# One layer with routed experts on one core: expert work issued in source order, and GpSimd partition broadcasts replaced by TensorE products

## The chip, the core and the metric

One core of one Trainium2 chip runs the whole program. The metric is device time in microseconds of one execution; lower is better. TensorE multiplies (its weight loads are recorded apart), VectorE and ScalarE do elementwise work, GpSimd does some of it and issues the scatters, SyncE (SP) issues the loads.

## The reference, cut to what matters

All of it is float32. 512 latent tokens and 256 context tokens of width 1024 go through a modulated norm, an input projection, a recurrent half (RG-LRU) and an attention half, an output projection with a gated residual, and a second modulated norm. Then comes the part that reads nearly all of the bytes: each of 16 experts takes the 64 tokens that it likes best.

```python
aff = jax.nn.softmax((h @ w_router).astype(jnp.float32), axis=-1)
g, idx = lax.top_k(jnp.swapaxes(aff, 1, 2), cap)          # cap = 64 of 512, 16 experts
xe = jax.vmap(lambda hb, ib: hb[ib])(h, idx)
...
return (jax.nn.silu(xk @ wg) * (xk @ wu)) @ wd            # 1024 -> 2816 -> 1024
...
jnp.zeros((n, D), yb.dtype).at[ib.reshape(-1)].add(yb.reshape(-1, D))
```

Each expert has three matrices of 1024 x 2816 values, 34.6 MB together, which are read once.

## The kernel before, in words

**Who orders the work.** Up to the first expert, instructions are not issued as they are written: a class `Flow` records them, and `flush` (line 224) orders them by a list schedule with costs written in the code and issues them in that order on each engine. All of them carry line 254 in the profile. A partition broadcast is costed there by its length alone (line 219). There are three flushes: norm 1 and the first chunk (line 574); projections, LRU, attention and the early half of the output projection (line 1007); the rest of the output projection, the second norm and the router (line 1098). A fourth (line 1241) takes the expert choice and the first expert's gathering, gate, up and gate-value products. The later experts are not recorded: they are issued as they are written, and the tile framework's own scheduler orders them, by line numbers 1152 to 1234.

**Broadcasts.** `gp.partition_broadcast` copies a row to all partitions on GpSimd at five places: `nlam` (line 633, the attention's lambda), the residual's gate row for the early token tiles (`residual_gate`, line 954, called at 1003 into a tile `qT` of the attention) and again for the late ones (line 1022, `m2row`), the router's bias `brt` (line 1034) and the row by which the experts' outputs are scaled (lines 1149 and 1150, into `brow`). GpSimd also makes `rs`, the reciprocal root of a token tile's mean square (`rstd`), for each of the four tiles, from a sum `s`: a scaling and a power. The router's logits `lg` of a tile need `rs`, `brt` and the router product `pl`; softmax, a transpose `pT` and the search for the 64 largest (`largest`, line 1069, rounds of 8 on VectorE, results `tops`, `last`, `least`) follow. Token tiles 0 and 1 are projected early, beside the attention; tiles 2 and 3 late (`late_proj`, line 1036), in two PSUM banks `po`.

**Loads.** The experts' weights go through a ring of 14 slots (line 351) of 128 x 3072 values. A slot holds 128 rows of gate or of up (`load_ex`, line 368), or three blocks of 128 rows of down (`load_dn`, line 1155); an expert takes 16 and 8 slots. SP issues them in order and waits at each for its slot. Two slots (`ring`) come free early, four (`r`) with the end of the attention, four (`ring`) with the output projection, two more after it, and the last two, for the seventh pair of gate and up rows, with `least`, the end of routing. From then on a slot comes free when TensorE has multiplied what is in it.

**An expert.** `gather` (line 1166) makes one-hot columns for the tokens of two experts and multiplies them with the tokens `X1` (TensorE, four products for each of eight blocks of 128 channels, alternating between two PSUM banks `y` and `tr`; ScalarE writes the block to `xe`). `up_part` (line 1202) multiplies, for each block k of 128 channels, the 64 token columns with 128 rows of gate and of up, in six chunks of up to 512 columns; gate goes to partitions 0 to 63 of a bank and up to 64 to 127. A float32 product is recorded as two TensorE records. In the recorded first expert, a bias in the code puts block k of gathering just ahead of block k of gate and up. `gates` (line 1184) gathers the gate values. `down_part` (line 1214) takes SiLU and product by chunk, four transposes each into `hT`, and then all 44 down products (two halves of the output by turns, into one bank `y`), the scaling to `ys`, and a scatter that adds to the output (line 1234, GpSimd).

Of the kernel before, what the change touches and what calls it, by code (L numbers as in the profile page):

```python
# [18 lines left out]
D = 1024  # L19
# [23 lines left out]
class Flow:  # L43
    """Records the instructions of a phase, orders them by a list schedule of their data
    dependences and issues them in that order; Tile still draws every wait."""
# [178 lines left out]
    def flush(self):  # L224
        """Issues what was recorded in the order of a list schedule, by the longest path to the end."""
# [87 lines left out]
def hybrid_block_kernel(ctx: ExitStack, tc: tile.TileContext, x, cx, w_ada, b_ada, w_in, w_out, w_router, w_gate,  # L313
# [23 lines left out]
    def carve(slot):  # L337
        """Small tiles out of a slot that the experts' weights take over."""
        flat, end = slot.rearrange("p a d -> p (a d)"), [0]

        def part(shape):
            n = int(np.prod(shape[1:]))
            v = flat[:shape[0], end[0]:end[0] + n]
            end[0] += n
            assert end[0] <= 3 * D
            dims = "abc"[:len(shape) - 1]
            return v if len(shape) == 2 else v.rearrange(f"p ({' '.join(dims)}) -> p {' '.join(dims)}",
                                                         **{d: k for d, k in zip(dims, shape[1:])})
        return part
# [18 lines left out]
    def load_ex(e, k, i):  # L368
        """Rows of an expert's gate (i = 0) or up weights."""
        s = slot().rearrange("p a d -> p (a d)")[:, :FE]  # L370
        sp.dma_start(s, (w_gate, w_up)[i][e, k * 128:(k + 1) * 128, :])
        return s
# [21 lines left out]
    def split(h, l, src):  # L394
        """src as the sum of two float32r parts."""
        copy(h, src)
        tt(l, src, h.bitcast(F32), OP.subtract)

# [12 lines left out]
    vec.tensor_copy(identr, ident)  # L411
    half = P0.tile([128, 8], F32)
# [47 lines left out]
    # start clears the accumulation flags of its whole bank, so only the first product in a bank sets it  # L460
    def chan_chunk(w, with_ctx, kouter=False):
        """Two channel tiles of 512 latent tokens, a bank each, and their 256 context tokens in a third one."""
# [119 lines left out]
    def tok_chunk(w, with_ctx):  # L582
        """256 columns of two token tiles to a bank."""
# [34 lines left out]
    # tables of the rotary embedding with the norms' gains, [token, tile, dim]  # L618
# [14 lines left out]
    gp.partition_broadcast(nlam, lsc[:, 67:68])  # L633
# [16 lines left out]
    # softplus(-lambda) as max(-lambda, 0) + 2 atanh(t / (2 + t)), t = exp(-|lambda|)  # L650
# [92 lines left out]
    def qk_post(v, t, tb, kind, dst):  # L743
        """Norm and rotation of token tiles t, t + 1 in bank v, 256 columns each; keys as float32r parts, transposed."""
# [194 lines left out]
    # w_out as two float32r parts in place of the input projection's operands  # L939
# [12 lines left out]
    def residual_gate(o):  # L952
        for i in range(2):
            gp.partition_broadcast(o[:, i * 512:(i + 1) * 512], brows[1][32 * i:32 * i + 1])
        return o
# [3 lines left out]
    def mix_parts(t, parts):  # L959
        """The mixer's output for token tile t as float32r parts; parts: (tiles of lru and att, H, L)."""  # L960
# [35 lines left out]
    for i in range(10):  # L996
        if i == 6:
            pre.append(load_ex(0, 0, 1))
        flow.boost = 10.0 if i >= 6 else 0.0
        next(at1)  # L1000
        flow.boost = 0.0
        if i == 6:
            m2e = residual_gate(AT.tile([128, D], F32, name="qT", tag="qT"))
        if i in (6, 8):
            early_proj((i - 6) // 2)
# [16 lines left out]
    m2l = residual_gate(RT.tile([128, D], F32, name="m2row"))  # L1022

    # logits = rstd * (x1 (A2 w)) + B2 w
# [5 lines left out]
    for k in range(KT):  # L1030
        pe.matmul(pB[:1, :NE], B2[:, k:k + 1], wrt[:, k], start=(k == 0), stop=(k == KT - 1))
    brt = RT.tile([128, NE], F32)
    copy(brt[:1], pB[:1, :NE])
    gp.partition_broadcast(brt, brt[:1])

    def late_proj(t):
        mh, ml = parts2 if t == 2 else mix_parts(t, ((KT, *(RT.tile([128, KT, 128], F32R, name=n) for n in ("mh", "ml"))),))
        out_proj(t, mh, ml, m2l, lambda: pd.tile([128, 512], F32, name="po", tag="po", bufs=2),
# [23 lines left out]
    # the 64 largest, sorted, of the first two tiles, then of these and the third tile, and of the fourth tile  # L1062
# [31 lines left out]
    # of two sorted rows the 64th largest is the largest of min(i-th of one, (64 - i)-th of the other)  # L1094
# [18 lines left out]
    # tokens above the least one taken, and of those equal to it the first ones, as many as are left to take  # L1113
# [15 lines left out]
    def count(o, m, stop):  # L1129
        """How many tokens up to each one have m, for each expert."""  # L1130
# [13 lines left out]
    # over the norms, by which the gathering products are scaled  # L1144
# [4 lines left out]
    gp.partition_broadcast(m5row, brows[2][96:97])  # L1149
    gp.partition_broadcast(m5row[:64], brows[2][64:65])  # L1150
# [15 lines left out]
    def gather(pair):  # L1166
        """The tokens of two experts, normed and modulated, one column each."""
        xe = E.tile([128, KT, 128], F32, name="xe", bufs=1)
# [5 lines left out]
        for k in range(KT):  # L1174
            flow.bias = 2050.0 - 100 * k
            pg = etr([128, 128]) if k % 2 else pe_ps.tile([128, 128], F32, name="y", tag="y", bufs=1)
            for t in range(4):
                pe.matmul(pg, X1[t][:, k * 128:(k + 1) * 128], oh[:, t].rearrange("p i s -> p (i s)"),  # L1178
                          start=(t == 0), stop=(t == 3))
            act.activation(xe[:, k], pg, AF.Identity, bias=B2[:, k:k + 1], scale=A2[:, k:k + 1])  # L1180
        flow.bias = 0.0
        return xe, oh

    def gates(pair, oh):
        """The gate values of the taken tokens of two experts (twice, below each other) and the tokens' numbers."""
# [16 lines left out]
    def up_part(xe, i, wgu):  # L1202
        gu = [pe_ps.tile([128, 512], F32, name="gu", tag="gu", bufs=6) for _ in FC]
        es = slice(i * CAP, (i + 1) * CAP)
        for k in range(KT):
            flow.bias = 2000.0 - 100 * k
            for (f, n), b in zip(FC, gu):
                for hh in range(2):
                    pe.matmul(b[hh * 64:(hh + 1) * 64, :n], xe[:, k, es], wgu[k][hh][:, f:f + n],  # L1209
                              start=(k == 0), stop=(k == KT - 1), skip_group_check=True)  # L1210
        flow.bias = 0.0
        return gu

    def down_part(gu, wd, g_t, ix):
        hT = E.tile([128, NF, CAP], F32, name="hT", tag="hT", bufs=1)
        y = pe_ps.tile([128, 512], F32, name="y", tag="y", bufs=1)
        for (f, n), b in zip(FC, gu):
# [7 lines left out]
        for ff in range(NF):  # L1225
            for hh in range(2):
                pe.matmul(y[hh * 64:(hh + 1) * 64, :], hT[:, ff], wd[ff][:, hh * 512:(hh + 1) * 512],  # L1227
                          start=(ff == 0), stop=(ff == NF - 1), skip_group_check=True)
# [7 lines left out]

    wgu, wd = load_gu(0), load_dn(0)
    xe, oh = gather(0)
    gu = up_part(xe, 0, wgu)
    gx = gates(0, oh)  # L1240
    flow.flush()
    act, vec, gp, pe, sp = nc.scalar, nc.vector, nc.gpsimd, nc.tensor, nc.sync
    down_part(gu, wd, *gx[0])
    for e in range(1, NE):
        wgu, wd = load_gu(e), load_dn(e)
        cur = gx[e % 2]
        gu = up_part(xe, e % 2, wgu)
        if e % 2 == 1 and e + 1 < NE:
            xe, oh = gather((e + 1) // 2)
            gx = gates((e + 1) // 2, oh)  # L1250
        down_part(gu, wd, *cur)
# [9 lines left out]
def _layout(inputs):  # L1261
    """The small parameters side by side, as the kernel loads them."""
# [4 lines left out]
    # [channel tile, block of the tile, in, direction, gate, out]  # L1267
# [37 lines left out]
```

## Time and profile before

| what | us |
|---|---|
| median of 3 runs | 1779.17 |
| lowest, highest | 1779.17, 1780.07 |
| span of the profiled execution, first to last instruction | 1780.5 |
| TensorE busy in it, matmuls | 1644.3 (92%) |
| VectorE, ScalarE, GpSimd busy | 387.6, 323.0, 132.5 |
| bytes moved by DMA | 607.33 MB, 341 GB/s over the span |

The profiled execution's own time is its span, 1780.5 us; it lies 1.3 us above the median. In the rows, PE is TensorE's matmuls, PEld its weight loads, DVE VectorE, ACT ScalarE, POOL GpSimd, SPq the queue of SyncE that issues loads. "<-" after idle time names what ended it; "issue" is idle time in which the engine waited for nothing that the profile shows. Names of tiles have lost their numbers, so `r` and `ring` each stand for several slots.

### The profile page before, as it was taken

The page shows a single profiled execution, that of the slowest core. Times are in us where ns is not written, and L with a number is a line of the kernel's source. Part 1 is how long each engine was busy: PE and PEld are TensorE (multiplying, and loading weights), DVE is VectorE, ACT ScalarE, POOL GpSimd, SP SyncE. Part 2 cuts the span into 40 slices and gives each one's busy share as a digit, 9 for nine tenths or more (in the row PEclk, how much of TensorE's full clock was granted, in tenths as well). Part 3 has the DMA queues.
Part 4 walks back from the last instruction along what each step waited for, and adds up shares of the span by engine and source line. Part 5 has one row for each costly group of instructions (what it writes and reads, how often), then busy time and mean ns, then how long its engine had stood idle before and what let it go on. Part 6 is the DMA issues. An engine that isn't in the chain of part 4 may idle for free.

```text
span 1780.5 us, 19112 instructions
## 1 busy us (share of the span) xinstructions
PE 1644.3 (92%) x8030; PEld 798.7 (45%) x8030; DVE 387.6 (22%) x788; ACT 323.0 (18%) x607; POOL 132.5 (7%) x143
## 2 busy tenths in 40 slices
PE   7999988883899999999999999999999999999997
PEld 4567787672433433344343334333433433343332
DVE  5667786724110100010010001010100010000001
ACT  5256755520010101020010102010100101020101
POOL 2141153300000000000000000000000000000000
PEclk9999999896899999999999999999999999999999
DMA  9563112255689999999999999999999999999997
GB/s 346 173 225 107 36 36 83 78 190 207 260 324 363 419 401 423 417 426 416 420 420 423 421 422 420 422 414 426 420 420 420 423 420 420 423 420 422 421 422 293
DMA packets 116900, 607.33 MB, mean 341 GB/s; under 512 B 12393, under 2 KB 31046, under 8 KB 84046
## 3 DMA queue, kind: packets, MB, share of 16 engines
q1 hardware_dynamic: 115534, 601.91, 83.1%
q0 software_dynamic: 1280, 4.20, 1.2%
q8 instruction: 63, 1.03, 0.2%
q14 instruction: 23, 0.19, 0.0%
HBM read 599.78 MB, written 6.29 MB: 340 GB/s over the span
## 4 chain that ended last, share of the span: by engine, by line
PE 49%; DMA 35%; issue 6%; DVE 6%; ACT 2%; POOL 1%; SPq 0%; POOLq 0%; ACTq 0%; DVEq 0%
PE gu L1209 18%; DMA r<-in_w_up_dram 16%; DMA ring<-in_w_up_dram 9%; PE y L1227 9%; PE ac L254 7%; DMA r<-in_w_down_dram 5%; PE gu L254 3%; DMA ring<-in_w_down_dram 3%; PE pv L254 3%; PE p L254 2%; PE tr L254 1%; PE tr L1223 1%; PE y L1178 1%; DVE ring L254 1%; PE tr L1178 1%
## 5 line engine op out<-in xcount | busy, mean ns | idle before, releaser
L1209 PE MATMUL gu<-r,xe 128*64 128x512 f32 (+1 forms) x1656 | 479.6, 560 | 5.9 <-DMA r<-in_w_up_dram 4.9
L1209 PE MATMUL gu<-ring,xe 128*64 128x512 f32 (+1 forms) x1224 | 365.8, 560 | 3.2 <-DMA ring<-in_w_up_dram 3.2
L1209 PEld LDWEIGHTS gu<-r,xe 128*64 128x64 f32 x1656 | 173.9, 137 | 275.9 <-issue 252.9
L1220 DVE TENSOR_TENSOR sg<-sg,gu 64x512 f32<-64x512 f32 x96 | 61.7, 647 | 785.3 <-ACT sg L1219 785.1
L1219 ACT ACTIVATE sg<-gu 64x512 f32<-64x512 f32 x96 | 52.7, 553 | 984.6 <-PE gu L1209 977.7
L1209 PEld LDWEIGHTS gu<-ring,xe 128*64 128x64 f32 x1224 | 131.4, 136 | 202.1 <-issue 187.1
L1227 PE MATMUL y<-r,hT 128*64 128x512 f32 x812 | 210.3, 617 | 0.6 <-DMA r<-in_w_down_dram 0.6
L1227 PE MATMUL y<-ring,hT 128*64 128x512 f32 x596 | 151.7, 606 | 1.2 <-DMA ring<-in_w_down_dram 1.2
L1234 POOL DMA_INDIRECT out_dram<-ys,ix x16 | 22.8, 1426 | 1313.2 <-DVE ys L1233 1313.2
L254 PE MATMUL ac<-w,ring 128*128 128x256 f32 x768 | 108.2, 290 | 1.1 <-DVE w L254 0.7
L1227 PEld LDWEIGHTS y<-r,hT 128*64 128x64 f32 x812 | 58.8, 139 | 99.3 <-issue 90.3
L254 PEld LDWEIGHTS ac<-w,ring 128*128 128x128 f32 x768 | 97.4, 190 | 12.8 <-issue 11.2
L1233 DVE SCALAR_TENSOR_TENSOR ys<-y,gate,brow 64x512 f32<-64x512 f32 x32 | 24.0, 749 | 294.9 <-PE y L1227 294.6
L1227 PEld LDWEIGHTS y<-ring,hT 128*64 128x64 f32 x596 | 43.7, 138 | 75.5 <-issue 69.0
L254 PE MATMUL ac<-ring,w 128*128 128x512 f32 (+1 forms) x240 | 68.4, 395 | 0.2 <-ACT V L254 0.2
L1223 PEld LDWEIGHTS tr<-ident,sg 64*128 64x128 f32 x352 | 30.5, 145 | 77.7 <-ACT hT L1224 40.6
L1223 PE MATMUL tr<-ident,sg 64*128 64x64 f32 x352 | 43.7, 244 | 13.8 <-ACT hT L1224 8.3
L1224 ACT ACTIVATE hT<-tr 128x256 f32<-128x256 f32 x96 | 35.1, 366 | 103.5 <-PE tr L1223 97.8
L254 PEld LDWEIGHTS ac<-ring,w 128*128 128x128 f32 x240 | 40.9, 194 | 8.6 <-issue 3.4
L1178 PE MATMUL y<-oh,raw 128*128 128x128 f32 x224 | 31.0, 281 | 14.6 <-DVE ys L1233 10.4
L254 ACT ACT_TABLE_LOAD x32 | 41.1, 1283 | 8.1 <-DVE lru L254 6.8
L254 PE MATMUL p<-kS,qs 128*128 128x256 f32 (+1 forms) x128 | 33.7, 378 | 5.4 <-ACT e L254 5.4
(250 smaller groups left out, 1263.7 us busy)
## 6 DMA issues: line engine op xcount, KB each, us to landing
r<-in_w_gate_dram SPq DMA_DIRECT2D x73, 1408.0 KB, 26.0
r<-in_w_up_dram SPq DMA_DIRECT2D x73, 1408.0 KB, 26.6
r<-in_w_down_dram SPq DMA_DIRECT2D x64, 1536.0 KB, 21.1
ring<-in_w_gate_dram SPq DMA_DIRECT2D x55, 1408.0 KB, 25.9
ring<-in_w_up_dram SPq DMA_DIRECT2D x55, 1408.0 KB, 26.5
ring<-in_w_down_dram SPq DMA_DIRECT2D x47, 1536.0 KB, 20.9
raw<-in_w_ada_dram SPq DMA_DIRECT2D x32, 512.0 KB, 4.7
raw<-in_w_in_dram SPq DMA_DIRECT2D x20, 512.0 KB, 4.7
```

The source lines that it names most:

```text
L254: getattr(self.eng[e], o["m"])(*o["a"], **o["k"])
L1178: pe.matmul(pg, X1[t][:, k * 128:(k + 1) * 128], oh[:, t].rearrange("p i s -> p (i s)"), start=(t == 0), stop=(t == 3))
L1209: pe.matmul(b[hh * 64:(hh + 1) * 64, :n], xe[:, k, es], wgu[k][hh][:, f:f + n], start=(k == 0), stop=(k == KT - 1), skip_group_check=True)
L1219: act.activation(sg[64:128, :n], b[:64, :n], AF.Silu)
L1220: vec.tensor_tensor(sg[64:128, :n], sg[64:128, :n], b[64:128, :n], op=OP.mult)
L1223: pe.transpose(pt[:, j], sg[64:128, j * 128:(j + 1) * 128], ident[64:128, 64:128])
L1224: act.activation(hT[:, f // 128:f // 128 + n // 128], pt[:, :n // 128], AF.Copy)
L1227: pe.matmul(y[hh * 64:(hh + 1) * 64, :], hT[:, ff], wd[ff][:, hh * 512:(hh + 1) * 512], start=(ff == 0), stop=(ff == NF - 1), skip_group_c ...
L1233: vec.scalar_tensor_tensor(ys[:, cs_], y[pp, :], g_t[pp, :], m5row[pp, :], op0=OP.mult, op1=OP.mult)
L1234: gp.indirect_dma_start(out=out, out_offset=bass.IndirectOffsetOnAxis(ap=ix[:, :1], axis=0), in_=ys, in_offset=None, compute_op=OP.add)
```

## The change

Partition broadcasts become products whose stationary operand is one column repeated: of ones for `nlam`, of the identity matrix for rows (it picks row p of a 128 x 512 tile), of the router's shift `B2` for the bias. The result stands in PSUM and is copied. The experts are no longer recorded, nor left to the framework: with `manual_schedule` they are issued in source order. For the first expert that is gathering of block k + 1 ahead of the gate and up products of block k, then the gate values. For the others it is all gate and up products, then (every second one) the gathering of the next two experts. In all, gate and up products of a chunk stand next to each other, and the down products of a chunk come after the transposes of the next one. Comments were also taken out.

```diff
+    ones = P0.tile([1, 128], F32)
+    vec.memset(ones, 1.0)
...
-    gp.partition_broadcast(nlam, lsc[:, 67:68])
+    pn = tr()
+    pe.matmul(pn[:, :1], ones, lsc[:, 67:68], start=True, stop=True)
+    vec.tensor_copy(nlam, pn[:, :1])
...
-    def residual_gate(o):
+    def row_to_all(o, r, p):
+        pe.matmul(o, ident[:, p:p + 1].to_broadcast([128, o.shape[0]]), brows[r], start=True, stop=True,
+                  skip_group_check=True)
+
+    def residual_gate(o, bank):
         for i in range(2):
-            gp.partition_broadcast(o[:, i * 512:(i + 1) * 512], brows[1][32 * i:32 * i + 1])
+            b = bank()
+            row_to_all(b, 1, 32 * i)
+            copy(o[:, i * 512:(i + 1) * 512], b)
         return o
...
-            m2e = residual_gate(AT.tile([128, D], F32, name="qT", tag="qT"))
+            m2e = residual_gate(AT.tile([128, D], F32, name="qT", tag="qT"), ac)
...
-    m2l = residual_gate(RT.tile([128, D], F32, name="m2row"))
+    def po_bank():
+        return pd.tile([128, 512], F32, name="po", tag="po", bufs=2)
+    m2l = residual_gate(RT.tile([128, D], F32, name="m2row"), po_bank)
...
-        pe.matmul(pB[:1, :NE], B2[:, k:k + 1], wrt[:, k], start=(k == 0), stop=(k == KT - 1))
+        pe.matmul(pB[:, :NE], B2[:, k:k + 1].to_broadcast([128, 128]), wrt[:, k], start=(k == 0), stop=(k == KT - 1))
     brt = RT.tile([128, NE], F32)
-    copy(brt[:1], pB[:1, :NE])
-    gp.partition_broadcast(brt, brt[:1])
+    copy(brt, pB[:, :NE])
...
     m5row = brow12[:, 0]
-    gp.partition_broadcast(m5row, brows[2][96:97])
-    gp.partition_broadcast(m5row[:64], brows[2][64:65])
+    p5 = pe_ps.tile([128, 512], F32, name="gu", tag="gu", bufs=6)
+    row_to_all(p5[:64], 2, 64)
+    row_to_all(p5[64:], 2, 96)
+    copy(m5row, p5)
...
-        for ff in range(NF):
-            for hh in range(2):
-                pe.matmul(y[hh * 64:(hh + 1) * 64, :], hT[:, ff], wd[ff][:, hh * 512:(hh + 1) * 512],
-                          start=(ff == 0), stop=(ff == NF - 1), skip_group_check=True)
+            if c:
+                products(*FC[c - 1])
+        products(*FC[-1])
...
     wgu, wd = load_gu(0), load_dn(0)
-    xe, oh = gather(0)
-    gu = up_part(xe, 0, wgu)
-    gx = gates(0, oh)
+    oh = one_hot(0)
     flow.flush()
     act, vec, gp, pe, sp = nc.scalar, nc.vector, nc.gpsimd, nc.tensor, nc.sync
-    down_part(gu, wd, *gx[0])
-    for e in range(1, NE):
-        wgu, wd = load_gu(e), load_dn(e)
-        cur = gx[e % 2]
-        gu = up_part(xe, e % 2, wgu)
-        if e % 2 == 1 and e + 1 < NE:
-            xe, oh = gather((e + 1) // 2)
-            gx = gates((e + 1) // 2, oh)
-        down_part(gu, wd, *cur)
+    with tc.manual_schedule():
+        for e in range(NE):
+            if e == 0:
+                xe, gu = new_xe(), banks()
+                gather(xe, oh, 0)
+                for k in range(KT):
+                    if k + 1 < KT:
+                        gather(xe, oh, k + 1)
+                    up_rows(gu, xe, 0, wgu, k)
+                gx = gates(0, oh)
+                cur = gx[0]
+            else:
+                wgu, wd = load_gu(e), load_dn(e)
+                cur = gx[e % 2]
+                gu = banks()
+                for k in range(KT):
+                    up_rows(gu, xe, e % 2, wgu, k)
+                if e % 2 == 1 and e + 1 < NE:
+                    oh = one_hot((e + 1) // 2)
+                    xe = new_xe()
+                    for k in range(KT):
+                        gather(xe, oh, k)
+                    gx = gates((e + 1) // 2, oh)
+            down_part(gu, wd, *cur)
```

`up_rows(gu, xe, i, wgu, k)` holds the inner loops of the old `up_part` for one block k (for each chunk of columns, gate then up), `gather(xe, oh, k)` those of the old `gather`, and `products(f, n)` the down products of one chunk.

## Rows read from the trace of the kernel before

**Rows 1.** The page's 40 slices of the span: DMA busy tenths, GB/s.
```profile
DMA  9563112255689999999999999999999999999997
GB/s 346 173 225 107 36 36 83 78 190 207 260 324 363 419 401 423 417 426 416 420 420 423 421 422 420 422 414 426 420 420 420 423 420 420 423 420 422 421 422 293
```

**Rows 2.** Windows: stretch, length, busy us of PE, PEld, DVE, ACT, POOL; clock, DMA share, GB/s.
```profile
448.00:541.00 93.00, 86.70 (x351) 38.38 (x353) 9.61 (x35) 10.45 (x21) 0.00 (x0) 0.91 0.75 288
541.00:660.00 119.00, 116.22 (x541) 48.12 (x539) 9.28 (x22) 9.06 (x20) 3.19 (x2) 0.97 1.00 409
...
995.00:1661.00 666.00, 639.08 (x2801) 250.90 (x2800) 50.67 (x104) 58.29 (x128) 11.22 (x8) 0.99 1.01 421
```

**Rows 3.** The chain of waits in order of time: start us, us, what.
```profile
417.91 15.06 DMA r<-in_w_up_dram
432.98 6.12 issue
...
1272.29 28.11 DMA ring<-in_w_up_dram
```

**Rows 4.** Waits of DVE in 380 to 450: total us, times, longest.
```profile
DVE lg L254 <- POOL rs L254: 27.4, 2, 20.8
...
DVE lg L254 <- POOL brt L254: 1.4, 1, 1.4
```

**Rows 5.** Timeline of POOL in 360 to 445: start, us, operation [idle before].
```profile
390.08 0.29 POOL L254 PARTITION_BROADCAST brt<-brt  x1 [7.71 <-issue]
401.98 0.18 POOL L254 TENSOR_SCALAR s<-s 128x1 f32<-128x1 f32 x1 [11.61 <-issue]
...
422.87 0.18 POOL L254 TENSOR_SCALAR s<-s 128x1 f32<-128x1 f32 x1 [13.17 <-issue]
431.03 0.80 POOL L254 PARTITION_BROADCAST brow<-brow  x1 [7.97 <-issue]
439.10 0.59 POOL L254 TENSOR_TENSOR rs<-s,half 128x1 f32<-128x1 f32 x1 [7.27 <-issue]
```

**Rows 6.** Timeline of SP's queue around the end of routing.
```profile
448.70 0.33 SPq L254 DMA_DIRECT2D r<-in_w_gate_dram  x1
...
464.29 0.33 SPq L254 DMA_DIRECT2D ring<-in_w_gate_dram  x1
```

**Rows 7.** Waits of DVE in 296 to 309.
```profile
DVE sums L254 <- POOL r L254: 4.3, 1, 4.3
```

**Rows 8.** Windows in the routing, columns as in rows 2.
```profile
396.00:406.00 10.00, 3.71 (x14) 2.52 (x14) 2.20 (x11) 0.84 (x6) 1.00 (x3) 0.66 0.09 38
...
414.00:421.00 7.00, 4.87 (x24) 4.41 (x24) 4.74 (x18) 2.64 (x6) 0.00 (x0) 0.66 0.99 356
```

**Rows 9.** Timeline of PE, projection to first expert: start, us to the last one's end.
```profile
373.39 7.86 PE L254 MATMUL po<-ring,w 128*128 128x512 f32 x33
...
385.49 0.55 PE L254 MATMUL pl<-wrt,B 128*1 128x16 f32 x16
...
417.27 2.84 PE L254 MATMUL pl<-wra,h2T 128*128 128x16 f32 x12
...
457.07 7.60 PE L254 MATMUL gu<-ring,xe 128*64 128x512 f32 x24
...
464.93 0.83 PE L254 MATMUL y<-oh,raw 128*128 128x128 f32 x6
...
501.76 4.94 PE L254 MATMUL gu<-r,xe 128*64 128x512 f32 x24
```

**Rows 10.** The page's groups (busy, mean ns | idle before) and loads (KB, us to landing).
```profile
L1223 PE MATMUL tr<-ident,sg 64*128 64x64 f32 x352 | 43.7, 244 | 13.8 <-ACT hT L1224 8.3
...
L1178 PE MATMUL y<-oh,raw 128*128 128x128 f32 x224 | 31.0, 281 | 14.6 <-DVE ys L1233 10.4
...
r<-in_w_gate_dram SPq DMA_DIRECT2D x73, 1408.0 KB, 26.0
```

**Rows 11.** The chain in 620 to 660, the second expert's down products.
```profile
624.32 15.16 PE y L1227 x69
```

**Rows 12.** The end of the span, timeline of all engines.
```profile
1774.32 1.40 POOL L1234 DMA_INDIRECT out_dram<-ys,ix  x1 [80.07 <-DVE ys L1233]
```

More of the change, by code (lines that the diff above doesn't have):

```diff
@@ L1030, in hybrid_block_kernel @@
     for k in range(KT):
-        pe.matmul(pB[:1, :NE], B2[:, k:k + 1], wrt[:, k], start=(k == 0), stop=(k == KT - 1))
+        pe.matmul(pB[:, :NE], B2[:, k:k + 1].to_broadcast([128, 128]), wrt[:, k], start=(k == 0), stop=(k == KT - 1))
     brt = RT.tile([128, NE], F32)
-    copy(brt[:1], pB[:1, :NE])
-    gp.partition_broadcast(brt, brt[:1])
+    copy(brt, pB[:, :NE])
     def late_proj(t):
         mh, ml = parts2 if t == 2 else mix_parts(t, ((KT, *(RT.tile([128, KT, 128], F32R, name=n) for n in ("mh", "ml"))),))
-        out_proj(t, mh, ml, m2l, lambda: pd.tile([128, 512], F32, name="po", tag="po", bufs=2),
+        out_proj(t, mh, ml, m2l, po_bank,
                  lambda: RT.tile([128, 512], F32, name="tm", tag="tm", bufs=2))
@@ L1164, in load_dn, with one_hot @@
         return res
-    def gather(pair):
-        xe = E.tile([128, KT, 128], F32, name="xe", bufs=1)
+    def one_hot(pair):
         oh = E.tile([128, 4, 2, CAP], F32, name="oh", bufs=1)
@@ L1173, in gather @@
                 vec.tensor_scalar(oh[:, t, i], slots, sl, rs2[:, t:t + 1], op0=OP.is_equal, op1=OP.mult)
[L1174 to L1182, printed above, removed]
+        return oh
+    def gather(xe, oh, k):
+        pg = etr([128, 128]) if k % 2 else pe_ps.tile([128, 128], F32, name="y", tag="y", bufs=1)
+        for t in range(4):
+            pe.matmul(pg, X1[t][:, k * 128:(k + 1) * 128], oh[:, t].rearrange("p i s -> p (i s)"),
+                      start=(t == 0), stop=(t == 3))
+        act.activation(xe[:, k], pg, AF.Identity, bias=B2[:, k:k + 1], scale=A2[:, k:k + 1])
     def gates(pair, oh):
@@ L1200, in hybrid_block_kernel, with banks, up_rows @@
     FC = [(f, min(512, FE - f)) for f in range(0, FE, 512)]
-    def up_part(xe, i, wgu):
-        gu = [pe_ps.tile([128, 512], F32, name="gu", tag="gu", bufs=6) for _ in FC]
+    def banks():
+        return [pe_ps.tile([128, 512], F32, name="gu", tag="gu", bufs=6) for _ in FC]
+    def up_rows(gu, xe, i, wgu, k):
         es = slice(i * CAP, (i + 1) * CAP)
-        for k in range(KT):
-            flow.bias = 2000.0 - 100 * k
-            for (f, n), b in zip(FC, gu):
-                for hh in range(2):
[L1209 to L1212, printed above, removed]
+        for (f, n), b in zip(FC, gu):
+            for hh in range(2):
+                pe.matmul(b[hh * 64:(hh + 1) * 64, :n], xe[:, k, es], wgu[k][hh][:, f:f + n],
+                          start=(k == 0), stop=(k == KT - 1), skip_group_check=True)
     def down_part(gu, wd, g_t, ix):
@@ L1216, in down_part, with products @@
         y = pe_ps.tile([128, 512], F32, name="y", tag="y", bufs=1)
-        for (f, n), b in zip(FC, gu):
+        def products(f, n):
+            for ff in range(f // 128, (f + n) // 128):
+                for hh in range(2):
+                    pe.matmul(y[hh * 64:(hh + 1) * 64, :], hT[:, ff], wd[ff][:, hh * 512:(hh + 1) * 512],
+                              start=(ff == 0), stop=(ff == NF - 1), skip_group_check=True)
+        for c, ((f, n), b) in enumerate(zip(FC, gu)):
             sg = E.tile([128, 512], F32, name="sg", bufs=2)
@@ L1224, in down_part @@
             act.activation(hT[:, f // 128:f // 128 + n // 128], pt[:, :n // 128], AF.Copy)
-        for ff in range(NF):
-            for hh in range(2):
-                pe.matmul(y[hh * 64:(hh + 1) * 64, :], hT[:, ff], wd[ff][:, hh * 512:(hh + 1) * 512],
-                          start=(ff == 0), stop=(ff == NF - 1), skip_group_check=True)
+            if c:
+                products(*FC[c - 1])
+        products(*FC[-1])
         ys = E.tile([128, NF, CAP], F32, name="ys", tag="hT", bufs=1)[:64].rearrange("p f c -> p (f c)")[:, :D]
@@ L1235, in down_part, with new_xe @@
                               in_offset=None, compute_op=OP.add)
+    def new_xe():
+        return E.tile([128, KT, 128], F32, name="xe", bufs=1)
     wgu, wd = load_gu(0), load_dn(0)
-    xe, oh = gather(0)
-    gu = up_part(xe, 0, wgu)
-    gx = gates(0, oh)
+    oh = one_hot(0)
     flow.flush()
     act, vec, gp, pe, sp = nc.scalar, nc.vector, nc.gpsimd, nc.tensor, nc.sync
-    down_part(gu, wd, *gx[0])
-    for e in range(1, NE):
-        wgu, wd = load_gu(e), load_dn(e)
-        cur = gx[e % 2]
-        gu = up_part(xe, e % 2, wgu)
-        if e % 2 == 1 and e + 1 < NE:
-            xe, oh = gather((e + 1) // 2)
-            gx = gates((e + 1) // 2, oh)
-        down_part(gu, wd, *cur)
+    with tc.manual_schedule():
[22 more added lines that the diff above has]
+            down_part(gu, wd, *cur)
     for p_ in (pe_ps, E, R3, R2, R0, R1, P0, X):
```

## The prediction

> **What bounds the kernel now.** First the slices. From about the twelfth on, the DMA engines are busy all the time at some 420 GB/s; between the fourth and the twelfth they are not [rows 1]. The windows say the same in numbers: 421 GB/s at 995 to 1661 us, but 288 at 448 to 541 and 409 at 541 to 660 [rows 2]. Then the chain of waits in order of time: late in the span it runs through weight loads back to back, and around 430 us it passes an idle stretch that ends in a GpSimd instruction [rows 3]. So two things are to be seen. The expert stage is a stream of 16 times 34.6 MB (three matrices of 1024 x 2816 x 4 bytes), 82.2 us each at 421 GB/s, and nothing on TensorE can shorten it. What can be shortened is the time in which this stream is not running at its full rate: before the stream, and in the first expert. Every microsecond of that comes off the end, because the loads after it are back to back.
>
> Two more views say why it isn't running. VectorE waited 27.4 us for `rs` and 1.4 us for `brt` in the routing [rows 4]. GpSimd's own timeline shows what it did meanwhile: around each partition broadcast it sits idle for 6 to 13 us with nothing that the profile shows ("issue"), once on the way in, once on the way out [rows 5]. The tiny `s` and `rs` operations behind it (0.2 and 0.6 us) wait in its queue; `rs` of the last token tile comes at 439.10. The slots of the seventh row pair of the first expert's gate and up are released by the end of routing, and SP issues them at 448.70 [rows 6]; I call that moment R.
>
> **The change, part by part: before R.** (a) `nlam` by a product and a copy: TensorE stands in order for a value that VectorE makes while TensorE is loading and multiplying other chunks; 0.3 us, at most some 2. (b) The residual row for the early projection. VectorE waits 4.3 us for GpSimd's copy `r` behind that broadcast, and all of it was on the chain [rows 7]. I take 4.0 off. (c) `m2row` and `brt`: the second broadcast held `rs` of the third tile for 6.6 us (27.4 less the long wait of 20.8), and `brt` for 1.4: 8.0 off [rows 4]. (d) In those pauses the granted clock fell: 3.71 us of matmuls at 0.66 of the clock in 396 to 406, 4.87 at 0.66 in 414 to 421 [rows 8]; at full clock they need about 2.4 and 3.2. VectorE's top-64 rounds run beside the second, so I take 2.0 off, not 3. (e) The wait of 20.8 us. Next late is TensorE's last router product, which ends at 417.27 + 2.84 = 420.1 [rows 9]; `lg` starts when `rs` ends, at 439.10 + 0.59 = 439.7 [rows 5], and can start at 420.2, so 19.5 off. VectorE's remaining rounds come after it as before.
>
> What is added: row products, each a 128 x 512 float32 product. The nearest rows are 33 `po` products in 7.86 us (0.24 each, one record a product) and 24 records for 12 gate and up products in 7.60 us, 0.63 a product [rows 9]; I take 0.9 with bounds 0.5 and 1.7. Two for the early row (1.8), two and a wait for a copy for the late one, as its banks are those of the late projection, which is queued behind (2.0). The router's bias product with 128 columns for 1: 16 records took 0.55; a router product with 128 columns took 0.24 a record in the stretch of low clock, so about 0.12 at full clock, and 16 of them 1.9: 1.3 more [rows 9]. The expert row's two products and its copy lie in TensorE's idle time during the top-64 rounds; without that cover they cost 0.9. Sum before R: -4.0 - 8.0 - 2.0 - 19.5 + 1.8 + 2.0 + 1.3 + 0.3 = -28.1, so R moves from 448.7 to 420.6. Bounds: the clock, the fit of the reordered list schedule and VectorE's crowding give 20 to 34.
>
> Such a pause has a price in the Trainium skill too: "GPSIMD Engine Reference", section 2.1, gives some 6 us for the first call of a freshly loaded kernel; it names no price for the way back. By that alone two loads, 12 us, would come off (c) and (e) where the rows have 27.5, and the forecast would be 1744. The rows decide, since they hold both ways.
>
> **After R.** Against 421 GB/s the stream lost 93 x (1 - 288/421) = 29.4 us in 448 to 541 and 119 x (1 - 409/421) = 3.4 in 541 to 660: 32.8 [rows 2]. The cause is TensorE: slots come free only as the first expert's row pairs are multiplied, and SP's next pair stands at 464.29, after the first [rows 6]. There a row pair took 7.60 us where the schedule put all gate products before the up products, but 4.94 where they alternate [rows 9]; records of 64 columns each then overlap in pairs. The gather of the next 128 rows adds about 1.2 (6 of its 8 records took 0.83 [rows 9]). So 8.8 us a pair before, 6.1 after, and a pair of loads of 1408 KB each [rows 10] needs 2.88 MB / 421 = 6.85. In source order the stream is thus the slower one from the second pair on. What stays: at R the pair before it is still landing (its load took 15.06 us from an issue at 417.91 [rows 3], which moves by some 8 to 410, so it lands at 425.1); that is 4.6 us of transfer not yet done at R, where before all had landed. The pair of R lands at 432.0. The first product pair starts 8.4 after R (448.70 to 457.07 [rows 6, 9]) and ends 4.94 later at 433.9; issue and first bytes by 436. So 4 us idle, and 2 for the rest. Gain 32.8 - 6 = 26.8, less 4.6.
>
> **Moved work that costs nothing, and its cover.** In the later experts, gate and up alternate too, the down products go between the transposes of the chunks, and the gather comes after all row pairs. TensorE then needs 8 x 4.94 = 39.5 for gate and up, 88 records at 15.16 / 69 = 0.22, so 19.3, for down [rows 11], 2.7 for transposes (43.7 / 16) and 4.4 for gathering (31.0 in one bank, as much in the other, over 14) [rows 10], with some 3 for the silu chain: 69 of 82.2 us. The cover is that slack of 13; if it were gone, each would be paid 16 times. The order of the loads on SP's queue stays, as does that of the scatters on GpSimd's. The last expert ends as before: the last load, its products, the scaling, the scatter at 1774.32 [rows 12].
>
> **Sum.** -28.1 + 4.6 - 26.8 = -50.3. Against the profiled span of 1780.5 that is 1730.2; this span lies 1.3 above the median of 1779.17, so I forecast **1729**.
>
> **The rivals.** (1) *The first expert gains nothing*: the pairs by turns don't overlap in source order, or the gather's two banks hold them up at 8.8 us a pair. Then -28.1 + 4.6, and 4 of the idle time right after R still go: 1752. Against it: the 4.94 pair, and the down products, which alternate in the same way. Chance 0.10. (2) *A next wait in routing* takes half of (b) to (e), VectorE being the candidate: R gains 14, the pair before it has landed, and the idle time after R shrinks as forecast: about 1738. Chance 0.14. (3) *Sooner than forecast*: R gains its upper bound of 34, the pair before it has landed by then, and the stream has no gap afterwards (32.8): 1712. Chance 0.06. (4) *Slower, by the clock.* TensorE, with 13 us of waiting in each expert, gets a lower clock. At a mean grant of 0.75, 69 us become 92, 9.8 over the stream, in 15 experts: 1729 + 147 = 1876. It decides from 69 / 82.2 = 0.84 downwards, and undoes the gain at about 0.81. Against it: a grant of 0.99 at 995 to 1661, where TensorE already waited for loads [rows 2], though less; and a slow TensorE has less idle time. Chance 0.04. "TensorE: Matmul & The Clock Gate", its part on HAM oscillation, in the Trainium skill is the rule that speaks for it: products that wait for DMA between short bursts fall back to half clock. No run here shows it yet in the expert stage. (5) *Nothing comes of it*, since the time goes to a reload that stays for another GpSimd operation and to TensorE's added products: 1779. Chance 0.03.
>
> **How the numbers follow.** The forecast has 0.63: its bounds (20 to 34 before R, 22 to 30 after it, less 4.6) make 1720 to 1742. Rivals 1 to 3 lie within 1710 to 1754, which I give as the range. A measurement can tell about 0.2% (3.6 us) from no change. Faster 0.93, same 0.03, slower 0.04.
>
> **What would show it.** Right: no long "issue" before GpSimd's small operations; `lg` of the last tile within a microsecond of its router product; R near 420; row pairs of the first expert near 5 us; 400 GB/s or more within 20 us of R; the expert stage at 421 as before, with more waiting on TensorE at a grant over 0.9. Wrong: a reload that stays, VectorE busy without a gap up to R at 430 or later, records of gate and up that don't overlap, or a clock under 0.84.

## The result, and the profile after

The median went from 1779.17 us to **1749.67** (four runs, 1747.86 to 1752.18); the ratio is 0.984, its 95% interval 0.983 to 0.986. The range held it and the direction was right, but 29.5 us came off where some 50 were forecast. The profiled execution's span is 1745.7 us against 1780.5, its own time 1747.86.

First the slices of the page of after, as in [rows 1].

```profile
PEclk9999999998999999999999999999999999999999
DMA  9573101238899999999999999999999999999996
GB/s 339 185 233 110 37 25 42 101 110 322 360 425 416 421 421 421 422 420 421 422 420 420 418 424 420 422 419 422 420 421 422 421 422 421 421 422 421 421 421 262
```

The load stream is at its full rate from the twelfth slice on, where before it stood at 324 in the twelfth and at 401 as late as the fifteenth [rows 1], so the hole after routing is closed. The fifth to seventh slices, the attention, are as empty as before: 37, 25 and 42 GB/s against 36, 36 and 83. The windows of after (columns as in [rows 2]) say the first thing in numbers:

```profile
434.00:541.00 107.00, 101.74 (x539) 43.73 (x541) 10.76 (x34) 10.47 (x21) 1.64 (x1) 0.95 0.97 397
541.00:660.00 119.00, 109.61 (x578) 43.62 (x576) 13.07 (x28) 14.70 (x32) 2.81 (x2) 0.96 1.02 420
995.00:1661.00 666.00, 557.63 (x2802) 217.74 (x2800) 50.40 (x104) 58.83 (x128) 11.23 (x8) 0.95 1.01 421
```

397 and 420 GB/s stand where 288 and 409 stood; the last row has the same 421 with 81 us less of TensorE busy. Its 557.63 of 666.00 us are 68.8 in the 82.2 of an expert, where 69 were forecast. GpSimd's timeline in the routing of after, to be read against [rows 5]:

```profile
375.11 0.19 POOL L254 TENSOR_SCALAR s<-s 128x1 f32<-128x1 f32 x1 [12.66 <-DVE s L254]
...
386.96 0.19 POOL L254 TENSOR_SCALAR s<-s 128x1 f32<-128x1 f32 x1 [0.54 <-DVE s L254]
...
401.87 0.19 POOL L254 TENSOR_SCALAR s<-s 128x1 f32<-128x1 f32 x1 [14.02 <-DVE s L254]
...
423.82 0.19 POOL L254 TENSOR_SCALAR s<-s 128x1 f32<-128x1 f32 x1 [20.93 <-DVE s L254]
424.09 0.56 POOL L254 TENSOR_TENSOR rs<-s,half 128x1 f32<-128x1 f32 x1
```

No "issue" is left: the idle time before each of these ends with VectorE's `s`, so GpSimd waits for data, and the last `rs` follows its `s` at once (0.3 us, where it was 16.2 [rows 5]). VectorE's waits in 370 to 436 for `lg` are now these alone, in place of 27.4 for `rs`:

```profile
DVE lg L254 <- PE pl L254: 2.6, 2, 1.3
```

SP's queue gives two times to hold against the trace of before: the first gate load of expert 0, late in the attention, and R.

```profile
302.20 0.33 SPq L254 DMA_DIRECT2D ring<-in_w_gate_dram  x1
...
434.10 0.33 SPq L254 DMA_DIRECT2D r<-in_w_gate_dram  x1
...
447.48 0.33 SPq L254 DMA_DIRECT2D ring<-in_w_gate_dram  x1
```

The first of them, and GpSimd's first `s`, stood here in the trace of before:

```profile
287.56 0.33 SPq L254 DMA_DIRECT2D ring<-in_w_gate_dram  x1
...
365.09 0.19 POOL L254 TENSOR_SCALAR s<-s 128x1 f32<-128x1 f32 x1 [11.94 <-DVE s L254]
```

The attention is **14.6 us later**, and nothing in the forecast had that. With GpSimd's four `s` and R as marks, the span of each profiled execution splits into stretches:

| stretch | before, us | after, us | difference | forecast |
|---|---|---|---|---|
| start to the first gate load | 287.56 | 302.20 | +14.6 | +0.3 |
| to the first `s` | 77.53 | 72.91 | -4.6 | -2.2 |
| first to fourth `s` | 57.78 | 48.71 | -9.1 | -6.7 |
| fourth `s` to R | 25.83 | 10.28 | -15.6 | -19.5 |
| R to the end | 1331.8 | 1311.6 | -20.2 | -22.2 |
| sum | 1780.5 | 1745.7 | -34.8 | -50.3 |

All that the change is about came within 4 us of its term; one stretch that it hardly touches took 14.6 back. Last, TensorE's timeline in the first expert of after:

```profile
442.51 4.94 PE L1224 MATMUL gu<-ring,xe 128*64 128x512 f32 x24
447.39 1.16 PE L1194 MATMUL y<-oh,raw 128*128 128x128 f32 x8
448.48 4.94 PE L1224 MATMUL gu<-r,xe 128*64 128x512 f32 x24
```

A row pair comes every 5.97 us, gathering included: less than the 6.85 that its load needs.

### The profile page after: what moved, and what is told of

It is laid out like the page before. It is cut to its first block, busy times and chain, and to the rows that moved or that the text cites. A ratio compares the mean times of both kernels' runs of the same rounds, so it can differ in the third digit from the quotient of the medians.

```text
span 1745.7 us, 19029 instructions
## 1 busy us (share of the span) xinstructions
PE 1487.1 (85%) x8044; PEld 724.6 (42%) x8044; DVE 387.6 (22%) x787; ACT 325.6 (19%) x608; POOL 133.0 (8%) x140
## 4 chain that ended last, share of the span: by engine, by line
DMA 54%; PE 21%; issue 5%; DVE 3%; ACT 1%; POOL 0%; POOLq 0%; SPq 0%; ACTq 0%; DVEq 0%
DMA r<-in_w_up_dram 22%; DMA ring<-in_w_up_dram 19%; PE gu L1224 8%; DMA ring<-in_w_down_dram 6%; DMA r<-in_w_down_dram 6%; PE y L1234 3%; PE ac L254 3%; PE y L1194 1%; PE po L254 1%; PE tr L1194 1%; PE tr L254 1%; PE tr L1243 1%; PE p L254 0%; DMA out_dram<-ys,ix 0%; PE pv L254 0%
## 5 line engine op out<-in xcount | busy, mean ns | idle before, releaser
L1224 PE MATMUL gu<-r,xe 128*64 128x512 f32 (+1 forms) x1752 | 395.2, 572 | 84.5 <-DMA r<-in_w_up_dram 80.4
L1224 PE MATMUL gu<-ring,xe 128*64 128x512 f32 (+1 forms) x1320 | 304.5, 573 | 60.1 <-DMA ring<-in_w_up_dram 57.9
L1224 PEld LDWEIGHTS gu<-r,xe 128*64 128x64 f32 x1752 | 133.4, 139 | 328.9 <-issue 206.4
L1224 PEld LDWEIGHTS gu<-ring,xe 128*64 128x64 f32 x1320 | 103.4, 139 | 242.8 <-issue 153.8
L1234 PE MATMUL y<-r,hT 128*64 128x512 f32 x812 | 201.7, 639 | 0.8 <-DMA r<-in_w_down_dram 0.8
L1234 PE MATMUL y<-ring,hT 128*64 128x512 f32 x596 | 148.1, 638 | 0.8 <-DMA ring<-in_w_down_dram 0.8
L254 PE MATMUL ac<-w,ring 128*128 128x256 f32 x768 | 103.7, 289 | 7.5 <-ACT ring L254 4.6
L1196 ACT ACTIVATE xe<-y,B,A 128x128 f32<-128x128 f32 x32 | 14.6, 457 | 464.6 <-PE y L1194 464.6
## 6 DMA issues: line engine op xcount, KB each, us to landing
ring<-in_w_up_dram SPq DMA_DIRECT2D x55, 1408.0 KB, 26.8
```

The source lines that it names most:

```text
L254: getattr(self.eng[e], o["m"])(*o["a"], **o["k"])
```

## The experiments

In all of them the computation is whole. Times are medians; the kernel before stood at 1776.73 us beside the first four and at 1777.83 beside the last four, but at 1779.17 beside after. So a difference between kernels of two of these groups is uncertain by some 2 to 3 us. Of the eight forecasts, the two of the halves apart missed (1759.14 and 1773.70, for 1752 and 1766 to 1769), and the other bank came sooner than forecast (1733.80 for 1738).

### What made the attention late?

The stretch holds two edits: `nlam` by a product into the bank `tr`, and the early residual row by products into a bank `ac`. Each can cost by what it does on the chip, or by the order in which the kernel's own list schedule puts the whole flush once the recorded instructions are others. The first kernel tells operation from order: it records the old broadcast, so that the list schedule sees what it saw, but issues product and copy in its place.

```diff
-                getattr(self.eng[e], o["m"])(*o["a"], **o["k"])
+                if o["m"] in self.instead:
+                    self.instead[o["m"]]()
+                else:
+                    getattr(self.eng[e], o["m"])(*o["a"], **o["k"])
...
     pn = tr()
-    pe.matmul(pn[:, :1], ones, lsc[:, 67:68], start=True, stop=True)
-    vec.tensor_copy(nlam, pn[:, :1])
+    gp.partition_broadcast(nlam, lsc[:, 67:68])
+
+    def as_product():
+        nc.tensor.matmul(pn[:, :1], ones, lsc[:, 67:68], start=True, stop=True)
+        nc.vector.tensor_copy(nlam, pn[:, :1])
+    flow.instead["partition_broadcast"] = as_product
```

> The changed kernel, with one thing different: the planner costs and orders nlam as the GpSimd broadcast that it was, and at that place in the order the product with the column of ones and its copy are issued. Theory P (the order that the list schedule finds, not the operations, made the attention part later): the second flush gets nearly the order of before, so the load of the first expert's first gate rows is issued near 290 us instead of 302.2, the routing ends (last two slots released) near 420 instead of 434.1, and the time is 12 to 15 us below the changed kernel's 1749.7: about 1736. Rival H (the product itself, in TensorE's queue in place of GpSimd's, stalls the attention part): the time stays at 1747 to 1752.

Measured: **1734.23 us**, 0.977 of before (0.975 to 0.979); R at 421.01. The product and the copy are there, and the attention's delay is gone:

```profile
289.32 0.33 SPq L258 DMA_DIRECT2D ring<-in_w_gate_dram  x1
```

The second takes `nlam` back to a broadcast (the row of ones goes with the product) and changes nothing else.

```diff
-    pn = tr()
-    pe.matmul(pn[:, :1], ones, lsc[:, 67:68], start=True, stop=True)
-    vec.tensor_copy(nlam, pn[:, :1])
+    gp.partition_broadcast(nlam, lsc[:, 67:68])
```

> The changed kernel with nlam alone made by the GpSimd broadcast again. Theory P: the order of the second flush is nearly that of before and the residual row by products keeps its gain, so 12 to 15 us below the changed kernel: about 1736, the same as with the order of before and the product issued (within 3 us), since GpSimd has nothing to do between 30 and 65 us that others wait for. Rival H: also some 1736, as the product is gone; it is told from P by the run that issues the product in the old order. Rival M (the early residual row's products in the two banks of the projection make the attention part later): 1747 to 1750.

Measured: **1733.70**, 0.976 (0.974 to 0.978); first gate load at 285.48, R at 421.87. The third takes the early residual row back instead.

```diff
-            m2e = residual_gate(AT.tile([128, D], F32, name="qT", tag="qT"), ac)
+            m2e = AT.tile([128, D], F32, name="qT", tag="qT")
+            for q in range(2):
+                gp.partition_broadcast(m2e[:, q * 512:(q + 1) * 512], brows[1][32 * q:32 * q + 1])
```

> The changed kernel with the early residual row alone (m2e) made by GpSimd broadcasts again; nlam by the product. Theory P: the bad order stays, and the wait of 4.3 us behind the broadcast comes back, less the 1.8 us of products: 1750 to 1756. Rival M (its products cause the later attention part): 1735 to 1740.

Measured: **1755.79**, 0.989 (0.987 to 0.991), 6 above the change itself; first gate load at 301.55. So the early row isn't the cause of the delay. The fourth keeps the product of `nlam`, but in another PSUM bank.

```diff
-    pn = tr()
+    pn = p2()[:, :512]
```

> The changed kernel with nlam's product in a score bank (p2, two buffers) in place of the transposes' one bank (tr, one buffer). Theory P says that what matters is the order the planner makes of it: its own costs put the end of the second flush at 314.1 us here, 329.2 in the changed kernel and 310.7 before, so the time should be 10 to 14 us below the changed kernel, near 1738. Rival H: the same time as the changed kernel, 1747 to 1752, since the same product stands in TensorE's queue.

Measured: **1733.80**, 0.977 (0.975 to 0.979); first gate load at 281.45, R at 418.52. One name of a bank is worth 16 us by the medians, 13 with each taken against the kernel before beside it.

The traces show the order itself. Up to 280 us the versions with the broadcast of `nlam`, here and below, and the one with the expert part alone have the same instructions in the same order on all four engines as the kernel before; the one that issues product and copy in its place differs by these and the row of ones alone. After keeps TensorE's order up to the product of `nlam`, which its list schedule put here, and has another one from there on:

```profile
115.66 0.38 PE L254 MATMUL tr<-ring,ones 1*128 1x1 f32 x2
```

In six executions in the old order, of as many kernels, the first gate load stood between 285.48 and 291.38 us; in three in the order of after, between 301.55 and 307.06; the other bank has an order of its own, and 281.45. The windows show what the new order does. In 150 to 310 us, columns as in [rows 2], after:

```profile
210.00:230.00 20.00, 12.94 (x78) 10.50 (x77) 8.70 (x19) 10.88 (x24) 3.27 (x6) 0.92 0.00 1
...
250.00:270.00 20.00, 13.99 (x97) 13.15 (x97) 17.79 (x24) 10.43 (x18) 14.46 (x14) 0.91 0.15 52
...
sum 160.00, PE 138.31 PEld 116.86 DVE 110.31 ACT 93.35 POOL 49.70; mean PE 17.29 PEld 14.61 DVE 13.79 ACT 11.67 POOL 6.21
```

And the same stretches where product and copy are issued in the old order:

```profile
210.00:230.00 20.00, 18.45 (x140) 16.87 (x140) 14.50 (x20) 13.43 (x19) 6.10 (x5) 1.00 0.14 49
...
250.00:270.00 20.00, 16.66 (x135) 15.64 (x134) 16.46 (x27) 8.66 (x18) 11.58 (x12) 1.00 0.17 53
...
sum 160.00, PE 146.50 PEld 125.68 DVE 129.58 ACT 104.44 POOL 55.21; mean PE 18.31 PEld 15.71 DVE 16.20 ACT 13.05 POOL 6.90
```

In those 160 us the plan of after leaves TensorE 8 us and VectorE 19 us less busy; the gaps are waits for other engines' work, the longest of TensorE's 4.6 us, and none is for the product of `nlam`. So the delay is the plan's. Shown is that it comes and goes with what the list schedule is given, at equal work on the chip. The list schedule's own costs had it already: they put the end of that flush at 329.2 us in after, against 310.7 before and 314.1 with the other bank, as the expectation of that run says. Why one product brings it to a plan that is worse by its own costs wasn't followed further.

### The two halves apart

The kernel before with the new expert part alone, the new `gather`, `up_rows` and `products` included:

```diff
-    xe, oh = gather(0)
-    gu = up_part(xe, 0, wgu)
-    gx = gates(0, oh)
+    oh = one_hot(0)
     flow.flush()
...
+    with tc.manual_schedule():
...
```

> The kernel before with the expert part of the change alone (source order, gate and up by turns); all broadcasts stay on GpSimd. Forecast's theory (the first expert holds the weight stream back by its pace, 8.8 us a row pair against 6.85 us for the loads): the end of routing stays at 448.7, and the 26.8 us that I put on the part after it come off, since nothing is still landing there: about 1752. Rival A (all of the change's gain in the expert part comes from an earlier end of routing): 1775 to 1780.

Measured: **1759.14**, 0.990 (0.988 to 0.993). And the products alone, with the expert part as before; the edit is against after:

```diff
-    oh = one_hot(0)
+    xe, oh = gather(0)
+    gu = up_part(xe, 0, wgu)
+    gx = gates(0, oh)
     flow.flush()
...
-    with tc.manual_schedule():
...
```

> The change's products in place of broadcasts alone, the expert part as before. Forecast's theory: the end of routing lies near 434, as in the changed kernel, the first expert takes 8.8 us a row pair again, so the gain is only the 14.6 us before the end of routing, less some 4 us of loads that haven't landed there: about 1766 to 1769. Rival B (a stream that starts earlier makes up for the first expert's pace): 1750.

Measured: **1773.70**, 0.998 (0.996 to 0.999), in ten runs from 1768.23 to 1780.06; that scatter is taken up at the end. The expert part alone brings 18.7 us, the products alone 4.1: their trace has the late attention too, with the first gate load at 307.06. With the delay undone, the products are worth 1759.14 - 1733.70 = 25.4 on top of the expert part. Alone, the halves sum to 22.8 where both together brought 29.5; these runs don't explain the rest, and the scatter of the single kernels is about as large.

### Where the first expert gains

The version with the broadcast `nlam` again (the edit is against it), and in the first expert all six gate products of a block ahead of its six up products, in source order all the same:

```diff
-                    up_rows(gu, xe, 0, wgu, k)
+                    for hh in range(2):
+                        for (f, n), b in zip(FC, gu):
+                            pe.matmul(b[hh * 64:(hh + 1) * 64, :n], xe[:, k, 0:CAP], wgu[k][hh][:, f:f + n],
+                                      start=(k == 0), stop=(k == KT - 1), skip_group_check=True)
```

> The kernel with nlam alone broadcast again (1733.7 us), with one more thing different: in the first expert, all gate products of a block come before its up products; order otherwise as in source. If the pairing of gate and up by turns is what the first expert gains: a row pair takes 9 to 10 us instead of 4.94 (no overlap at all: 24 records at twice the step), so some 10 us a pair with the gather against 6.85 for the loads, 8 pairs: 20 to 30 us above 1733.7, 1754 to 1764. If it is the place of the gathering and the down products: within 4 us of 1733.7.

Measured: **1760.47**, 0.990 (0.989 to 0.992): 26.8 more than with the two by turns. TensorE's timeline in it:

```profile
442.66 1.16 PE L1190 MATMUL y<-oh,raw 128*128 128x128 f32 x8
443.75 8.43 PE L1269 MATMUL gu<-r,xe 128*64 128x512 f32 x24
```

Its windows, columns as in [rows 2]:

```profile
434.00:480.00 46.00, 46.00 (x151) 17.93 (x150) 0.00 (x0) 1.83 (x4) 0.00 (x0) 0.98 0.76 280
480.00:541.00 61.00, 57.66 (x261) 22.16 (x261) 7.69 (x20) 7.72 (x15) 1.77 (x1) 0.94 0.81 324
```

And the same windows of the version with the broadcast `nlam` and the products by turns:

```profile
434.00:480.00 46.00, 44.47 (x265) 19.50 (x262) 1.12 (x5) 4.62 (x8) 0.00 (x0) 1.00 0.93 371
480.00:541.00 61.00, 59.19 (x288) 21.12 (x290) 6.56 (x15) 4.93 (x11) 1.77 (x1) 0.94 1.01 420
```

The same 24 records take 8.43 us in place of 4.94, at a clock of 0.98 in the first window. With gathering that is 9.5 us a pair, above the load's 6.85: TensorE sets the pace again, at 280 GB/s. That the work is issued in source order brings nothing here by itself; the turns do.

### The order in the later experts

Again with the broadcast `nlam`; the first expert by turns, the other fifteen left to the framework's scheduler.

```diff
-    with tc.manual_schedule():
-        for e in range(NE):
...
+    with tc.manual_schedule():
+        xe, gu = new_xe(), banks()
...
+    for e in range(1, NE):
...
```

> The kernel with nlam alone broadcast again (1733.7 us), with the later 15 experts left to the framework's scheduler as in the kernel before; only the first stays in source order. Forecast's theory (the later experts are bound by the weight stream, so their order is worth nothing): within 4 us of 1733.7. Rival C (source order in the later experts is worth something, or costs something by a starved TensorE): over 5 us above, or below, 1733.7.

Measured: **1734.72**, 0.975 (0.973 to 0.978): no difference from 1733.70. Windows of it and of after differ by TensorE alone, here in the version left to the framework:

```profile
995.00:1661.00 666.00, 633.22 (x2804) 252.16 (x2800) 50.66 (x104) 58.36 (x128) 11.23 (x8) 0.99 1.02 421
```

633 or 558 us busy of 666, at the same 421 GB/s: the loads set the pace either way.

### R, and what comes after it

| kernel | R, us | span, us | R to the end |
|---|---|---|---|
| before | 448.70 | 1780.5 | 1331.8 |
| products only | 445.59 | 1778.3 | 1332.7 |
| gate, then up (`nlam` broadcast) | 424.27 | 1759.7 | 1335.4 |
| after | 434.10 | 1745.7 | 1311.6 |
| early row broadcast | 440.00 | 1751.7 | 1311.7 |
| experts only | 441.20 | 1752.2 | 1311.0 |
| first expert only (`nlam` broadcast) | 427.67 | 1739.5 | 1311.8 |
| `nlam` broadcast | 421.87 | 1734.0 | 1312.1 |
| `nlam` issued as products, planned as broadcast | 421.01 | 1731.6 | 1310.6 |
| `nlam` in another bank | 418.52 | 1730.7 | 1312.2 |

The last column has two values, 1331.8 to 1335.4 without the turns in the first expert and 1310.6 to 1312.2 with them, wherever R lies. So the forecast's two parts, time up to R and time after it, do add in these traces, and what differs between the versions with the turns is R alone. Three versions at 1733.7 to 1734.2 beat both kernels; the smallest edit is the other bank for `nlam`.

## Why the prediction was right in direction and 20 us short

**The step that failed** is part (a): "`nlam` by a product and a copy: TensorE stands in order for a value that VectorE makes while TensorE is loading and multiplying other chunks; 0.3 us, at most some 2." As the price of the operation this holds: with the old plan and the product issued, 1734.23 against 1733.70 with the broadcast. But the edit also changes the input of the list schedule, which orders the whole flush anew, and that cost 14.6 us at the first gate load and 1749.67 - 1733.70 = 16.0 in the median (13.5 with each taken against the kernel before beside it). The bounds had "the fit of the reordered list schedule", but only within 20 to 34 us for R; R gained 14.6, outside them. Rival 2 gave R that figure by another mechanism, a next wait in the routing; the routing had none. The forecast's own bounds, 1720 to 1742, miss the median. The range held it because rivals 1 to 3 had widened it, and none of their mechanisms occurred: that it was held is luck.

**(b) The early row** came as forecast or better: 4.6 us between the first gate load and the first `s`, where 2.2 were forecast. The traces of two other versions with that broadcast took 74.8 and 74.7 us there, against 77.5 before and 72.9 after, so 1.8 to 4.6 is what they give. Undone alone it costs 6.1 in the median (1755.79 against 1749.67), but in the traces 4.8 of R's 5.9 lie between the third and the fourth `s`, in the stretch of the last section.

**(c), (d), the late row and (e)** gave 24.6 us from the first `s` to R, where 26.2 were forecast. The table's split at the fourth `s` misleads, since that mark itself stood behind a pause in the trace of before: VectorE had made the sum by 417.3, and GpSimd scaled it at 422.87, after 13.17 us of "issue" [rows 5]. In after, GpSimd follows VectorE by 0.2 us. VectorE's two sums, before and after:

```profile
417.16 0.13 DVE L254 TENSOR_TENSOR s<-s 128x1 f32<-128x1 f32 x1
```

```profile
423.59 0.14 DVE L254 TENSOR_TENSOR s<-s 128x1 f32<-128x1 f32 x1
```

Split there, (e) gave 31.5 - 10.5 = 21.0 us for 19.5: the pauses went, as the rows said. The last router product now ends at 424.01 + 1.06 = 425.07, and `lg` follows at 425.91, within the microsecond of the forecast.

```profile
424.01 1.06 PE L254 MATMUL pl<-wra,h2T 128*128 128x16 f32 x8 [0.39 <-ACT h2T L254]
```

(c), (d) and the late row then gave 3.6 for 6.7. How much of that is the clock's part, (d), the traces don't separate; it isn't safe, as the last section shows.

The Trainium skill's "GPSIMD Engine Reference", section 2.1, prices only the first call of a freshly loaded kernel, at some 6 us; an estimate by that page, with 12 us for two of them in place of 27.5, would have the same stretch gain about 11. The 24.6 that came speak for the pauses on the way back too.

**After R**: 20.2 for 22.2, and the cause is the one named: 4.94 us a pair by turns, 8.43 without, which is 23.3 us of the time after R (1335.4 - 1312.1) and 26.8 in the median. Rival 1, no gain in the first expert, falls with it.

**Rival 4, the clock**: TensorE waits for loads more than before. In 995 to 1661 of after, the largest two groups are these, where before had 3.7 and 2.8 us:

```profile
PE gu L1224 <- DMA r<-in_w_up_dram: 48.0, 26, 2.7
PE gu L1224 <- DMA ring<-in_w_up_dram: 32.2, 18, 2.9
```

The granted clock over the same stretch was 0.95 (0.99 before), well above the 0.84 from which it would decide. The rule in the Trainium skill, "TensorE: Matmul & The Clock Gate", on HAM oscillation, has products that wait for DMA between short bursts fall back to half clock; the trace doesn't show it here, with single waits of up to 2.9 us. Whether longer ones would bring it, no run here shows.

**The rest of the gap.** By spans 50.3 - 34.8 = 15.5 us are missing, and 14.6 - 0.3 of them are (a). By medians 20.7 are missing: the median of after lies 4.0 above this execution's span (2.2 of it is time outside the span), that of before 1.3 below its own. With (a) mended the median is 1733.7, 4.7 above the forecast; against the kernel before beside it, that is 43.0 of the 50.2 forecast.

## What to carry to other kernels

Where a planner orders the code, an edit costs what its instruction costs plus what the new plan costs. The two come apart if the new instruction is issued in the place that the plan gave the old one, and it pays to try another buffer before giving up an edit, and to read the plan's own end before building: here it had the delay. Where a stream of loads fills the rest of the span, split the time at the last event that the stream waits for: time up to it, and time after it, add, and each edit can be tested on one of the two. Float32 products of 64 columns into the two halves of a bank belonged next to each other here: the row pair took 4.94 us where all of one half and then the other took 8.43.

## What was not expected of the hardware

The granted clock fell while TensorE was busy, and not in the same way in every execution. In after, 392 to 412 us and on, columns as in [rows 2]:

```profile
392.00:402.00 10.00, 10.00 (x60) 8.58 (x58) 2.84 (x5) 1.52 (x5) 0.13 (x1) 1.00 0.90 377
402.00:412.00 10.00, 10.00 (x65) 9.03 (x65) 4.55 (x21) 4.65 (x11) 0.80 (x3) 0.83 0.49 174
```

The same work with the products only, from the same point (the third `s` less 10 us):

```profile
397.00:407.00 10.00, 10.00 (x60) 8.63 (x58) 2.83 (x5) 1.52 (x5) 0.33 (x2) 0.98 0.94 393
407.00:417.00 10.00, 10.00 (x46) 9.45 (x46) 1.79 (x9) 4.36 (x9) 0.60 (x2) 0.50 0.45 160
```

TensorE is busy throughout in both, with 60 records in the first window, and the second window then gets 0.83 or 0.50; 0.50 is the lower of the two levels, 1.2 GHz. What it does there is router products of 16 columns between transposes and parts of the late projection. From the third to the fourth `s` it took 21.95 us in after and with `nlam` in another bank, 23.53 where the product was issued in the old plan, 26.8 in four other executions and 28.34 with the products only. So part (d) of the forecast, 2.0 us for a clock that no longer falls in pauses, can't be counted on: it falls without a pause too.

Nor is this the only such stretch. Three of the traces have the same instructions in the same order up to R: `nlam` broadcast, gate then up, and first expert only. They took 26.8 us each between the third and fourth `s`, and 136.3 to 136.4 from the first gate load to R; yet R lies at 421.87, 424.27 and 427.67, since that load stands at 285.48, 287.88 and 291.38. Most of it arises at 60 to 66 us, where in part a load lands later and the granted clock differs again (columns as in [rows 2], the three in that order):

```profile
60.00:64.00 4.00, 3.19 (x19) 2.04 (x19) 4.00 (x16) 0.21 (x1) 0.00 (x0) 1.00 0.87 303
```

```profile
60.00:64.00 4.00, 3.33 (x10) 1.54 (x10) 4.00 (x15) 0.21 (x1) 0.00 (x0) 0.52 0.91 323
```

```profile
60.00:64.00 4.00, 2.37 (x8) 1.52 (x10) 4.00 (x18) 0.29 (x2) 0.00 (x0) 0.50 0.92 327
```

After and the products only, also of one order up to R, differ in both places: by 4.9 us at the first gate load and by 6.4 between the third and fourth `s`. So one execution's R can lie 6 us, once 11.5, from another's with the same instructions, and a difference of that size between two traces is not yet an effect of an edit. That is about the scatter among runs of one kernel (1747.86 to 1752.18 for after, 1768.23 to 1780.06 for the products only). Why the clock differed among them, no run here shows.
